# Reading the DeltaNet's triangular systems from plain scratch with six loads a step, and handing out no late modulation at the end of the attention

## The chip, the cores and the metric

The kernel runs on one core of one Trainium2 chip. The metric is the time of one execution in device microseconds (us). Before the change it is 1784.63 us, the median of 3 runs (1782.84 to 1789.32).

The core's engines run side by side, each through its own list of instructions in order: TensorE (PE, matmuls; PEld is its loading of weights), VectorE (DVE), ScalarE (ACT) and GpSimd (POOL). The queue of SyncE (SP) and that of ScalarE issue the transfers (DMAs).

## What is computed

One layer over 256 latent tokens and 256 context tokens of width 2048, in fp32. Cut to what matters here:

```python
sh1, sc1, g1, sh2, sc2, g2 = split(silu(c) @ w_ada + b_ada, 6)     # and the same for c_ctx
(lq_a, lkv_a, lk_r, ldq, ldk, ldv, ldz, lda, ldb, lga, lgb) = split_columns(
    modulate(rmsnorm(x, norm_mix), sh1, sc1) @ w_in)               # and the same for ctx
...
y_mla_l = attend_latent(q_l, k_l, v_l, k_c, v_c)
o_dn_c, s_ctx = dn_bidirectional(cq, ck, cv, cgd, cbeta, s_zero, not last)
o_dn_l, _ = dn_bidirectional(lq, lk, lv, lgd, lbeta, s_ctx, True)
y_l = merge_branches(y_mla_l, dn_output(o_dn_l, ldz, dn_o_norm, x.dtype), lga, lgb, w_o_mla, w_o_dn, w_out)
x = x + g1 * y_l
x = x + g2 * conv_glu(modulate(rmsnorm(x, norm_ffn), sh2, sc2), w_ffn_up, ffn_conv, w_ffn_down)
```

The part that the change touches is the gated DeltaNet. For each of 8 heads, 2 directions and 8 chunks of 64 tokens (4 of the context, 4 latent) it solves one unit lower triangular system of size 64:

```python
kb = k * beta
m = where(strict, einsum('bhnid,bhnjd->bhnij', kb, k) * decay, 0.0)
rhs = concatenate([v * beta, kb * exp(gc)[..., None]], axis=-1)
sol = triangular_solve(m + eye(c), rhs, left_side=True, lower=True, unit_diagonal=True)
u, w = sol[..., :dv], sol[..., dv:]
...
def step(s, inp):
    v_new = u_c - einsum('bhcd,bhde->bhce', w_c, s)
    s_next = s * g_c + einsum('bhcd,bhce->bhde', k_c, v_new)
    o = einsum('bhcd,bhde->bhce', q_c, s) + einsum('bhcj,bhje->bhce', a_c, v_new)
    return s_next, o
```

## The kernel before, in words

**Weights.** Every weight block of 128x1024 comes from HBM in fp32 (512 KB, tile `raw`), through a ring of NR = 8 tiles. ScalarE casts it to a high part (`whi`, L123), VectorE subtracts that from it for a low part (`wlo`, L124), and TensorE multiplies with both, from rings of NH = 6. A weight can be requested as soon as a `raw` tile is free, and the requests stand in SP's queue in the order in which they were planned. The 128 blocks of the "late modulation" (`rawa`, the four of the six modulation vectors that are not needed at the start) go through the same ring.

**Order.** TensorE's order is pinned to the program's; ScalarE's, VectorE's and SP's follow the scheduler except where they are pinned. A transfer counts up one of eight completion counters when it lands. The transfers of SP's queue and of ScalarE's queue take these eight in turn, and a transfer whose counter was last given to one still under way waits for that one: the rows of the order below show it as a wait for DMAHW0 to DMAHW7.

**The stages, with the times of the profile.** (1) The start, to 35 us: SP loads the vectors, x (`xl`) and the context (`xc`), then 16 MB of scale weights (`wt`) and 16 MB of shift weights (`raw<-in_wadab`), of each of which the first parts are needed first. TensorE adds up the squares (`pss`, the norms), the shifts (`amp`), and then projects (`fp`, `mmp`). ScalarE's copy of `amp` leads to `shs`, which gives the modulated input `h` of the first projection. (2) The DeltaNet's heads, to about 440 us. They leave, for each of the 128 systems (4x32), its two 32x32 diagonal blocks in scratch in HBM (`Ud`) and the block below the diagonal (`Uo`). (3) The attention, from about 440 to 740 us, in four pairs of heads, `b = 0` to 3, each with 7 rounds `n`. Its own work is handed out in pieces (`mla_project`, `mla_attend`). With every piece of estimated cost `c`, `side(c, r)` hands out other work that is due: `fill` (the projections of z and of the gates, tiles `raw<-in_wz` and `in_wgm`), `inv` (the triangular systems) and `ada` (the late modulation, AD = 0.55 of the cost). In the last pair the ratio is 2.0 for fill and inv, and behind the loop stands one more call, `side(2600, 1.0)`. (4) The scan over the eight chunks, about 735 to 890 us, with the attention's out projection (`branch`) and the gate tiles between its steps, and `ada` at ADS = 0.3 of the cost. (5) The out projection, the norm and the feed-forward, to the end. `ada` is handed out there too, until all four quarters are done.

**The systems.** `inverse()` loads `Ud` into `ux` and solves the diagonal blocks on VectorE. It then stores them: 8 transfers to `Xq` (L846, for each of four groups of partitions the transposed first block `xt` and the second block), and 16 transfers to `Tt` (L851), in which each system stands as it will be multiplied, as a 64x64 matrix in two 32x32 diagonal blocks: pieces of 32 numbers, 128 bytes. `ux` lives in a pool that is closed behind it, and its place in memory is given to tiles of the attention. `off_diagonal()` then takes the systems in eight steps: it loads `uo` (from `Uo`) and the two inverse diagonal blocks `xd` (from `Xq`, L869), multiplies them (`ivp`), and stores the block beside the diagonal to `Tt`, in 4 transfers a step from SP (L892). The fourth block of each system is zero: it is written to `Tt` at the start from a small zero tile `none`, in two transfers of 2048 pieces from ScalarE's queue (L656). In the scan, `load_system` (L1273) loads a step's 16 systems into `tt` with one transfer, 128 rows of 2 KB; two tiles `tt` are used in turn. TensorE's `yp` multiplies with them.

**The attention's keys.** `k_norm` (L1029) sums the squares of a key tile over the partitions (`ks`: TensorE, from ScalarE's `ksq`), and VectorE makes `km` from it (L1035). In the first pair `km` lies where `ux` lay.

**The late modulation.** `ada_rest()` loads 128 blocks `rawa` (L262) and multiplies each with the spread conditioning vector on VectorE, summing along the row (L281; the same operation appears under L68 where its place was pinned). Two loads are requested ahead of the product. They form four quarters of 32 products (`ada.done` counts them), of which the first must be complete ahead of the out projection (`wout`) and the third ahead of the feed-forward.

**What the change touches**: L101 and L102, L653 to L656, `inverse()` L846 to L851, `off_diagonal()` L869 and L892, `side` (L1179), its two calls (L1209 and L1212), the scan's tiles (L1259) and `load_system` (L1273). In the changed kernel the same lines stand 2 to 11 lower: L127 there is L129 here, L842 is L846, L860 is L869, L1269 is L1273.

## Time and profile before

| | |
|---|---|
| median of 3 runs | 1784.63 us (1782.84 to 1789.32) |
| the profiled execution | 1786.89 us |
| its span in the trace | 1785.1 us |
| TensorE's mean granted clock | 0.985 |
| TensorE matmul (PE) busy | 1737.5 us |
| TensorE weight load (PEld) busy | 1507.2 us |
| VectorE (DVE) busy | 1356.8 us |
| ScalarE (ACT) busy | 950.5 us |
| GpSimd (POOL) busy | 41.4 us |
| moved by DMA | 417.15 MB, HBM 232 GB/s over the span |

How to read the rows in the prediction. A row that begins with two numbers is of the timeline: the time from the span's start, the duration (us), the engine, the line, the operation, the tile that is written and the tiles read. A number with an arrow in brackets is the idle time of the engine ahead of it and what ended it. A row "A <- B: total, times, longest" is of the waits: what A waited for B in all, how often, and the longest. A row that begins with two times and a colon is a stretch: its length, then the busy time of PE, PEld, DVE, ACT and POOL in it with the number of instructions, the granted clock, the mean busy share of the 16 DMA engines, and GB/s. Rows with "min/median/max" are of one line's or one tile's instructions: count, durations in ns, first and last time. L68 is the line of a helper through which the pinned instructions of all engines go, so these are told apart by their tiles.

### The profile page before, as it was taken

How to read it: one execution, taken by the hardware profiler on the slowest of the kernel's cores; microseconds unless marked ns; L12 is line 12 of the kernel's file. 1: busy time of each engine (PE TensorE's matmuls, PEld its weight loads, DVE VectorE, ACT ScalarE, POOL GpSimd, SP SyncE). 2: the span in 40 equal slices, each digit the busy share in tenths (PEclk: the TensorE clock that was granted, in tenths of full speed). 3: DMA queues.
4: the chain of work that ended last, by engine and by line, in shares of the span. 5: the costliest groups of instructions: out<-in, count | busy, mean ns of one | idle time of the engine just before them, and what ended most of it. 6: DMA issues, size and time to landing. Idle time of an engine off the chain costs nothing.

```text
span 1785.1 us, 34155 instructions
## 1 busy us (share of the span) xinstructions
PE 1737.5 (97%) x12957; PEld 1507.2 (84%) x12957; DVE 1356.8 (76%) x2696; ACT 950.5 (53%) x1966; POOL 41.4 (2%) x48
## 2 busy tenths in 40 slices
PE   7999999999799999999999999999999999999999
PEld 5887888888688888788878888888888888888888
DVE  4677799879578879787779979887788887655554
ACT  3335454454477766665646546555555555544443
POOL 0000011000000000000010000000000000000000
PEclk8999999999899999999989999999999999999999
DMA  9992588783578868999647968776667776666662
GB/s 348 407 373 93 150 235 249 230 257 109 138 255 248 260 214 273 360 339 361 233 130 233 328 199 281 232 237 207 202 219 229 228 225 201 182 198 199 198 199 87
DMA packets 190260, 417.15 MB, mean 234 GB/s; under 512 B 56912, under 2 KB 95696, under 8 KB 187792
## 3 DMA queue, kind: packets, MB, share of 16 engines
q1 hardware_dynamic: 165024, 401.59, 68.7%
q10 hardware_dynamic: 25072, 13.39, 2.5%
q8 instruction: 101, 1.65, 0.4%
q14 instruction: 63, 0.52, 0.1%
HBM read 387.00 MB, written 27.79 MB: 232 GB/s over the span
## 4 chain that ended last, share of the span: by engine, by line
PE 63%; issue 8%; DMA 1%; DVE 1%; ACT 0%; SPq 0%; POOL 0%; POOLq 0%; DVEq 0%
PE fps L68 27%; PE dps L68 13%; PE gtp L68 11%; PE brp L68 3%; PE vps L68 1%; PE kps L68 1%; PE qps L68 1%; PE sps L68 1%; PE kp L68 1%; PE ivp L68 1%; PE op L68 1%; PE yps L68 1%; PE yp L68 0%; DMA YM<-Ys 0%; SPq L851 0%
## 5 line engine op out<-in xcount | busy, mean ns | idle before, releaser
L123 ACT CAST whi<-raw 128x512 fp32r<-128x512 f32 (+1 forms) x940 | 578.9, 620 | 413.6 <-PE dps L68 113.5
L124 DVE TENSOR_TENSOR wlo<-raw,whi 128x512 fp32r<-128x512 f32 (+1 forms) x940 | 637.3, 686 | 211.4 <-ACT whi L123 203.5
L68 PE MATMUL fps<-H,whi 128*128 128x512 f32 x1376 | 475.0, 394 | 3.1 <-DVE H L1472 3.1
L68 PE MATMUL fps<-H,wlo 128*128 128x256 f32 x1376 | 372.3, 280 | 0.0
L68 PEld LDWEIGHTS fps<-H,whi 128*128 128x128 f32 x1376 | 253.7, 189 | 54.7 <-issue 1.9
L68 PEld LDWEIGHTS fps<-H,wlo 128*128 128x128 f32 x1376 | 259.7, 189 | 7.5 <-DVE wlo L124 0.5
L68 PE MATMUL gtp<-h,whi 128*128 128x512 f32 x640 | 231.4, 399 | 0.0
L68 PE MATMUL mmp<-h,whi 128*128 128x512 f32 x640 | 229.5, 400 | 0.0
L68 PE MATMUL dps<-GB,whi 128*128 128x512 f32 (+1 forms) x595 | 195.7, 377 | 0.0
L68 PE MATMUL mmp<-h,wlo 128*128 128x256 f32 x640 | 177.5, 283 | 0.0
L68 PE MATMUL gtp<-h,wlo 128*128 128x256 f32 x640 | 173.9, 282 | 0.0
L68 PE MATMUL dps<-GB,wlo 128*128 128x256 f32 x560 | 155.2, 282 | 0.0
L68 PEld LDWEIGHTS gtp<-h,whi 128*128 128x128 f32 x640 | 120.5, 190 | 25.3 <-issue 0.9
L68 PEld LDWEIGHTS mmp<-h,whi 128*128 128x128 f32 x640 | 119.8, 189 | 24.9 <-ACT dkx L531 0.3
L68 PEld LDWEIGHTS dps<-GB,whi 128*128 128x128 f32 x595 | 109.2, 188 | 20.2
L68 PEld LDWEIGHTS gtp<-h,wlo 128*128 128x128 f32 x640 | 121.5, 190 | 4.5
L68 PEld LDWEIGHTS mmp<-h,wlo 128*128 128x128 f32 x640 | 121.8, 190 | 3.6 <-issue 1.4
L68 PEld LDWEIGHTS dps<-GB,wlo 128*128 128x128 f32 x560 | 105.8, 189 | 0.6
L281 DVE CUSTOM_DVE_ANT_0 rawa<-rawa,sch 128x1024 f32<-128x1024 f32 x68 | 82.9, 1222 | 20.9 <-DMA rawa<-in_wada 19.4
L68 PE MATMUL fp<-h,gh 128*128 128x256 f32 (+1 forms) x448 | 85.5, 291 | 2.5 <-ACT h L68 1.7
L68 PEld LDWEIGHTS fp<-h,gh 128*128 128x128 f32 (+1 forms) x448 | 69.7, 190 | 7.6 <-issue 4.1
L68 DVE CUSTOM_DVE_ANT_0 rawa<-rawa,sch 128x1024 f32<-128x1024 f32 x60 | 72.9, 1218 | 0.0
(574 smaller groups left out, 2563.4 us busy)
## 6 DMA issues: line engine op xcount, KB each, us to landing
rawa<-in_wada SPq DMA_DIRECT2D x128, 512.0 KB, 5.2
raw<-in_wgate SPq DMA_DIRECT2D x82, 512.0 KB, 4.4
raw<-in_wval SPq DMA_DIRECT2D x82, 512.0 KB, 4.6
raw<-in_wdown SPq DMA_DIRECT2D x80, 512.0 KB, 4.2
wt<-in_wadas SPq DMA_DIRECT2D x16, 1024.0 KB, 9.6
raw<-in_wadab SPq DMA_DIRECT2D x32, 512.0 KB, 11.6
raw<-in_wgm SPq DMA_DIRECT2D x32, 512.0 KB, 5.6
raw<-in_wgd SPq DMA_DIRECT2D x32, 512.0 KB, 6.9
```

The costliest lines, as they stand in the source:

```text
L68: i = f(*a, **k)
L123: act.copy(hi, raw)
L124: dve.tensor_tensor(out=lo, in0=raw, in1=hi, op=ALU.subtract)
L281: (odve if ada.bound else dve).tensor_tensor_reduce(out=w, in0=w, in1=sch, scale=1.0, scalar=0.0, op0=ALU.mult, op1=ALU.add, accum_out=par ...
```

## The change

The scratch `Tt` is dropped, and with it the zero tile, the two zero fills at the start, the 16 transfers behind `inverse()` and the 4 a step in `off_diagonal()`. `Xq` gets a third plane: the transposed first block, the first block as it is, and the second. That makes 12 transfers behind `inverse()`; `off_diagonal()` reads planes 0 and 2. Its result goes to a new scratch `Xo` in one transfer a step, from ScalarE's queue. In the scan two `tt` tiles are zeroed once on GpSimd, and `load_system` fills the three blocks of each system with six transfers of 32 KB (two directions by three blocks; 256 pieces of 128 bytes each), from `Xq[1]`, `Xq[2]` and `Xo`. And `side` has a flag `late` that leaves out `ada`: it is set for `b == 3 and n > 3`, which is three of the seven rounds (4, 5 and 6) of the last pair, and for the call behind the loop. The two edits are independent of each other, and no computation is changed.

```diff
--- before.py
+++ after.py
@@ -98,8 +98,6 @@
     make_identity(nc, ident)
     ones = const.tile([P, 1], F32, name="ones")
     dve.memset(ones, 1.0)
-    none = const.tile([P, 32], F32, name="none")
-    pool.memset(none, 0.0)
     onesr = const.tile([P, P], F32R, name="onesr")
     dve.tensor_copy(onesr, ones.broadcast_to([P, P]))
     half = const.tile([P, 1], F32, name="half")
@@ -650,10 +648,8 @@
     Ud = dram.tile([4, 32, 2, 32, 32], F32, name="Ud")
     Uo = dram.tile([4, 32, 32, 32], F32, name="Uo")
 
-    Xq = dram.tile([2, 32, 4, 32, 32], F32, name="Xq")
-    Tt = dram.tile([P, 16, 4, 64], F32, name="Tt")
-    for d in range(2):
-        act.dma_start(Tt[64 * d + 32 : 64 * d + 64, :, :, 0:32].rearrange("c s g j -> c (s g) j"), none[:32].unsqueeze(1).broadcast_to([32, 64, 32]))
+    Xq = dram.tile([3, 32, 4, 32, 32], F32, name="Xq")
+    Xo = dram.tile([32, 4, 32, 32], F32, name="Xo")
     As = dram.tile([4, P, 8, 64], F32, name="As")
     conv = mid.tile([P, 24, 3], F32, name="conv")
     dve.tensor_scalar(out=conv, in0=off["dn_conv"].rearrange("p (f w) -> p f w", w=3), scalar1=0.5, scalar2=None, op0=ALU.mult)
@@ -842,13 +838,8 @@
         act.copy(xt, X[:, 0].rearrange("p c j -> p j c"))
         for g in range(4):
             gs = slice(32 * g, 32 * g + 32)
-            for n, x in enumerate((xt, X[:, 1])):
+            for n, x in enumerate((xt, X[:, 0], X[:, 1])):
                 sync.dma_start(Xq[n, :, g], x[gs])
-        for g in range(4):
-            for d in range(2):
-                for b in range(2):
-                    rs = slice(64 * d + 32 * b, 64 * d + 32 * b + 32)
-                    sync.dma_start(Tt[rs, :, g, 32 * b : 32 * b + 32].rearrange("c s j -> s c j"), X[32 * g + 16 * d : 32 * g + 16 * d + 16, b])
         yield 1000
         pI.close()
 
@@ -866,7 +857,7 @@
             sync.dma_start(uo, Uo[:, :, rs].rearrange("g j r i -> (g j) r i"))
             xd = pi.tile([P, 2, 4, 32], F32, tag="xd", name="xd", bufs=2)
             for n in range(2):
-                sync.dma_start(xd[:, n], Xq[n, rs].rearrange("r g j c -> (g j) r c"))
+                sync.dma_start(xd[:, n], Xq[2 * n, rs].rearrange("r g j c -> (g j) r c"))
             return uo, xd
 
         ahead = load(0)
@@ -887,9 +878,7 @@
                 if n == 0:
                     yield OC / 2
             act.copy(uo, ip)
-            for g in range(4):
-                dst = Tt[64 * (q // 4) : 64 * (q // 4) + 32, 4 * (q % 4) : 4 * (q % 4) + 4, g, 32:64]
-                sync.dma_start(dst, uo[32 * g : 32 * g + 32])
+            act.dma_start(Xo[4 * q : 4 * q + 4].rearrange("r g c i -> (g c) r i"), uo)
             yield OC / 2
         pI.close()
 
@@ -1176,10 +1165,11 @@
     pairs = {}
     ryx = mid.tile([P, 2, T], F32, tag="krd", name="ryx")
 
-    def side(c, r):
+    def side(c, r, late=False):
         fill(r * c)
         inv(r * c)
-        ada(AD * c)
+        if not late:
+            ada(AD * c)
 
     pe.pinned = True
     for c in mla_project(0):
@@ -1206,10 +1196,10 @@
             for st in (pr, tail, at):
                 c = next(st, None)
                 if c is not None:
-                    side(c, R1 if b < 3 else 2.0)
+                    side(c, R1 if b < 3 else 2.0, b == 3 and n > 3)
             next(back, None)
         tail = at
-    side(2600, 1.0)
+    side(2600, 1.0, True)
     for _ in tail:
         pass
     inv.finish()
@@ -1258,6 +1248,8 @@
         jit = ps1.tile([P, 6, 1024], F32, name="jit")
         TTv = [ps1.tile([P, HEADS, 64], F32, name=f"tt{n}") for n in range(2)]
         av = ps1.tile([P, HEADS, 64], F32, name="av")
+        for n in range(2):
+            pool.memset(TTv[n], 0.0)
         half_ = [slice(0, 64), slice(64, 128)]
         S = ps1.tile([P, HEADS, 2, P], F32, name="S")
         steps = (4, 5, 6, 7, 0, 1, 2, 3)
@@ -1270,7 +1262,11 @@
 
         def load_system(n):
             st, tt = steps[n], TTv[n % 2]
-            sync.dma_start(tt, Tt[:, 2 * st : 2 * st + 2].rearrange("p a g j -> p (a g) j"))
+            for d in range(2):
+                for r, c, x in ((0, 0, Xq[1]), (32, 32, Xq[2]), (0, 32, Xo)):
+                    rs, cs = slice(64 * d + r, 64 * d + r + 32), slice(c, c + 32)
+                    n = 16 * d + 2 * st
+                    sync.dma_start(tt[rs, :, cs], x[n : n + 2].rearrange("a g c i -> c (a g) i"))
             return tt
 
         def load_ke(n):
```

How the instructions move is told by the order of each engine. A row names the line, the operation, the tile written, the tile read and its size; brackets hold the completion counters or engines that it must wait for by the program. The first place is the start of ScalarE's queue, where the zero fills stood. Before:

```order
L306 DMA cv<-in_cv 128x32
L321 DMA sel<-in_sel 128x3
L656 DMA Tt<-none 2048x1x32 [waits Pool_49]
L309 ACT_TABLE_LOAD
L309 ACTIVATE cth<-cv 128x32 [waits DMAHW0_49]
L68 ACTIVATE sq<-xl 128x4x256 [waits DMAHW3_49]
L68 ACTIVATE sq<-xl 128x4x256 [waits DMAHW6_49]
L656 DMA Tt<-none 2048x1x32
```

The same place now:

```order
L304 DMA cv<-in_cv 128x32
L319 DMA sel<-in_sel 128x3
L307 ACT_TABLE_LOAD
L307 ACTIVATE cth<-cv 128x32 [waits DMAHW0_49]
L68 ACTIVATE sq<-xl 128x4x256 [waits DMAHW3_49]
L68 ACTIVATE sq<-xl 128x4x256 [waits DMAHW5_49]
```

Both fills are gone from ScalarE's queue; as they took two of the eight counters in turn, the counters of all later transfers of both queues change. The second place is SP's queue at the end of `inverse()`, from its last copies to `Xq` on. `raw<-in_wz` is a weight of the z projection, `xd` what `off_diagonal()` reads. Before:

```order
L846 DMA Xq<-xt 32x1024
L846 DMA Xq<-ux 32x1024
L851 DMA Tt<-ux 16x32x32 x16
L869 DMA xd<-Xq 128x4x32 x4
L129 DMA raw<-in_wz 128x1024
L262 DMA rawa<-in_wada 128x1024
L129 DMA raw<-in_wqb 128x1024
```

The same place now:

```order
L842 DMA Xq<-ux 32x1024 x2
L842 DMA Xq<-xt 32x1024
L842 DMA Xq<-ux 32x1024 x2
L860 DMA xd<-Xq 128x4x32 x2
L127 DMA raw<-in_wz 128x1024
L860 DMA xd<-Xq 128x4x32 x2
L260 DMA rawa<-in_wada 128x1024
```

The 16 transfers from `ux` to `Tt` no longer stand ahead of `xd` and of the weights; the weight of z is requested between the loads of `xd`. The third place is SP's queue at the head of the scan: `jit` are its keys and values, `tt` its systems. Before:

```order
L1267 DMA jit<-KTs 128x1024
L1268 DMA jit<-Vs 128x1024
L1273 DMA tt_8909<-Tt 128x512
L1278 DMA jit<-KEs 128x1024
L1267 DMA jit<-KTs 128x1024
L1268 DMA jit<-Vs 128x1024
```

The same place now:

```order
L1259 DMA jit<-KTs 128x1024
L1260 DMA jit<-Vs 128x1024
L1269 DMA tt_8860<-Xq 32x8x32 x2
L1269 DMA tt_8860<-Xo 32x8x32
L1269 DMA tt_8860<-Xq 32x8x32 x2
L1269 DMA tt_8860<-Xo 32x8x32
L1274 DMA jit<-KEs 128x1024
L1259 DMA jit<-KTs 128x1024
```

Six transfers stand where one stood, in the first and in each later step. TensorE's order is the same before and after.

## Prediction

> **What bounds the kernel now.** I read the page first, then the waits of TensorE, then its busy time by stretches, and then the timeline at each stretch where it stands.
>
> ```profile
> PE 1737.5 (97%) x12957; PEld 1507.2 (84%) x12957; DVE 1356.8 (76%) x2696; ACT 950.5 (53%) x1966; POOL 41.4 (2%) x48
> PE ks L68 <- DVE km L1035: 6.5, 1, 6.5
> PE pss L68 <- DVE sq L68: 4.9, 4, 3.9
> PE yps L68 <- DVE PT L124: 3.5, 1, 3.5
> 500.00:550.00 50.00, 50.00 (x412) 44.18 (x411) 40.65 (x91) 36.15 (x86) 3.50 (x3) 1.00 0.80 251
> ```
>
> TensorE is busy 97% of the span. No matmul is added, dropped or reordered, so only its idle time and the slow-clock time behind it can change. Where nothing stands out (500 to 550), it is busy 50.00 of 50. The idle time is 1785.1 - 1737.5 = 47.6 us, and these three waits, 14.9 of it, lie where the change works: the start (`pss`), the first keys (`ks`) and the end of the attention (`yps`).
>
> **The start: two zero fills go.** The queue of SP loads x (`xl`) and the context (`xc`), then what modulation and the first projection need. The first row is SP's waits, the next six the timeline, the last two the stretches (mean clock, DMA share, GB/s at the end).
>
> ```profile
> SPq L68 <- DMA Tt<-none: 9.7, 1, 9.7
> 5.57 0.33 SPq L68 DMA_DIRECT2D xl<-in_xT  x1
> 15.58 0.33 SPq L68 DMA_DIRECT2D xc<-in_ctxT  x1
> 21.14 1.81 PE L68 MATMUL pss<-sq,ones 128*32 128x512 f32 x8 [3.90 <-DVE sq L68]
> 30.60 1.93 PE L68 MATMUL amp<-raw,csf 128*32 128x256 f32 x32
> 33.45 0.42 ACT L68 ACTIVATE shs<-amp,vecs 128x2 f32<-128x2 f32 x2 [0.43 <-PE amp L68]
> 35.13 0.53 PE L68 MATMUL fp<-h,gh 128*96 128x256 f32 x1 [1.75 <-ACT h L68]
> 16.00:18.00 2.00, 1.24 (x12) 0.97 (x8) 0.00 (x0) 0.15 (x1) 0.00 (x0) 1.00 0.80 153
> 30.00:35.00 5.00, 2.42 (x64) 1.50 (x64) 1.17 (x3) 2.88 (x9) 0.00 (x0) 1.00 1.03 426
> ```
>
> The last quarter of the context is issued at 15.58, though the load ahead of it went at 5.57: SP waits 9.7 us until the first zero fill, issued from ScalarE's queue, has landed. VectorE squares that quarter for `pss`, so TensorE stands 3.90. SP's order shows why: loads of both queues take eight completion counters in turn, and that load's counter is the fill's. Before, then after:
>
> ```order
> L68 DMA xl<-in_xT 128x1024 [waits DMAHW2_49]
> L68 DMA xc<-in_ctxT 128x1024 [waits DMAHW4_49]
> L68 DMA wt<-in_wadas 128x2048 [waits DMAHW5_49]
> ```
>
> ```order
> L68 DMA xl<-in_xT 128x1024 [waits DMAHW1_49]
> L68 DMA xc<-in_ctxT 128x1024 [waits DMAHW2_49]
> L68 DMA wt<-in_wadas 128x2048 [waits DMAHW3_49]
> ```
>
> The load now waits for the counter of a small early load and can go at about 6. From there the start is a matter of bytes: the last shift weights stand behind 8.6 MB (x and context 4.2, scale weights 2.1, shift weights 2.1, vectors 0.2). At about 0.41 MB/us, a little under the 426 GB/s row, from 2 us on, they are in by 23; with an estimated tail of 1 to 1.5 us (the smallest landing below is 1.9 with its issue) it is 24 to 24.5. Now they end with the `amp` matmuls at 30.60 to 32.5; then those would end at about 25.5. The chain from there to the first projection (`shs` at 33.45, `fp` at 35.13) is the same. That is 7 us early; I take 6.5, since loads for later steps are led by a little less. The lower bound is 4, the wait of 3.9 alone; the upper 7.5.
>
> **The first keys: 16 writes of Tt go.** The solved diagonal blocks lie in `ux`. Before, SP stores them to Xq in 8 writes and to Tt in 16 of 128-byte pieces. The first four rows are the timeline, then the stretches around it.
>
> ```profile
> 460.33 17.87 SPq L851 DMA_DIRECT2D Tt<-ux  x16
> 480.60 0.16 DVE L1035 SCALAR_TENSOR_TENSOR km<-ks,krm 128x4 f32<-128x4 f32 x1 [10.91 <-DMA xd<-Xq]
> 480.91 0.60 PE L68 MATMUL ks<-ones,ksq 128*32 128x1 f32 x32 [6.51 <-DVE km L1035]
> 485.75 0.62 ACT L123 CAST whi<-raw 128x512 fp32r<-128x512 f32 x1 [12.81 <-DMA raw<-in_wz]
> 469.00:471.30 2.30, 0.11 (x3) 0.01 (x2) 0.69 (x2) 1.19 (x4) 0.00 (x0) 1.00 0.08 27
> 471.30:474.40 3.10, 3.10 (x44) 2.79 (x44) 0.00 (x0) 1.49 (x3) 0.00 (x0) 0.59 0.28 49
> 474.40:480.90 6.50, 0.01 (x1) 0.02 (x1) 0.30 (x2) 0.00 (x0) 0.00 (x0) 0.50 0.70 89
> 480.90:485.50 4.60, 4.59 (x49) 4.39 (x50) 2.67 (x7) 0.00 (x0) 2.01 (x2) 0.50 0.88 222
> L846 SPq DMA_DIRECT2D Xq<-ux x4: 339/418/436, 454.0 to 459.9; - x4
> DMA to landing us min/median/max: 1.9/2.7/3.2
> ```
>
> VectorE's `km` is the first tile to reuse the place of `ux`, and so waits for all reads of it. TensorE makes its sums from 471.3, so it could run at 471.9, but it runs at 480.60, when the last Tt write has landed (the row names the transfer that came nearest). TensorE's second `ks` stands behind it for 6.51 us. The weights of z are queued behind the same writes, and ScalarE idles 12.81 us for them. On SP, after the change (before, the 16 Tt rows stand where the third Xq copy ends and `xd` begins):
>
> ```order
> L842 DMA Xq<-ux 32x1024 [waits DMAHW2_49]
> L842 DMA Xq<-ux 32x1024 [waits DMAHW3_49]
> L860 DMA xd<-Xq 128x4x32 [waits DMAHW5_49,DMAHW4_49,DMAHW0_49]
> L860 DMA xd<-Xq 128x4x32
> L127 DMA raw<-in_wz 128x1024 [waits DMAHW6_49,DVE_49]
> ```
>
> Eight Xq writes go between 454.0 and 459.9; four more at 0.42 us end at about 462 and land 2.7 later, before 465. Then `km` runs at 471.9, under TensorE's twelve `vps` matmuls (to 474.4), and the second `ks` follows with no gap: 6.5 us off the path. The weights of z go out at about 465 instead of 480.88 and are in before TensorE needs them at about 480. What is late next is the wait of 2.2 us ahead of the first `ks` (the stretch from 469): ScalarE's order there is the same, so it stays. The clock: after it the granted clock is 0.59 for 3.1 us, then 0.50 for 4.6 us after the big wait, which costs 1.3 + 2.3 = 3.6 us. I leave 2 us of that for the wait that stays (4 us at half clock), so 1.5 more is saved. The term is 8.0 us; bounds 6.5 and 6.5 + 3.6 = 10.1.
>
> The Trainium skill, "TensorE: Matmul & The Clock Gate" (What's actually happening), says that the clock halves after an idle window of about 3.4 us. By that rule the stall of 2.2 us alone would not slow it and this term would be 10.1 us, the sum 15.6; here the clock fell to 0.59 within 3 us of that stall, which speaks against it.
>
> **Tt's last columns: 32 writes become 8 on ScalarE's queue.** SP loses 32 issues where TensorE has no gap (500 to 550), so nothing is gained. ScalarE gets 8 issues, and SP can wait for one of them on a shared counter.
>
> ```profile
> L910 ACTq DMA_DIRECT2D Gs<-zx x18: 326/326/333, 550.5 to 735.5; - x18
> SPq L262 <- DMA Gs<-zx: 3.9, 1, 3.9
> ```
>
> 8 x 0.33 = 2.6 us of ScalarE beside 36 of 50 busy; at worst one SP wait of 3.9. I take 0.5 us, between 0 and 3.9.
>
> **The scan: 48 loads in place of 8.** Each of 8 steps read 128 pieces of 2 KB; now it reads 6 x 256 = 1536 pieces of 128 bytes. The nearest rows for such pieces are the Tt writes (window 461 to 478); then the old loads, their first use, a zeroing of tiles as large as the new one, SP's largest waits in the scan, a load and the use of what it brings, and two stretches.
>
> ```profile
> q1 hardware_dynamic: 7156, 1.06, 46.9%
> L1273 SPq DMA_DIRECT2D tt<-Tt x8: 319/326/510, 721.7 to 845.1; - x8
> L68 PE MATMUL yp<-jit,tt x32: 269/269/320, 739.6 to 740.4; 64*64 64x128 f32 x32
> 437.50 0.99 POOL L861 MEMSET bd<- 128x512 f32 x2 [38.61 <-PE mmp L68]
> SPq L129 <- DVE wlo L124: 31.2, 21, 4.8
> SPq L1267 <- PE kp L68: 21.3, 5, 6.9
> 742.08 0.42 SPq L1273 DMA_DIRECT2D tt<-Tt  x1
> 779.85 1.03 PE yp L68 x32
> 740.00:760.00 20.00, 20.00 (x203) 17.07 (x192) 15.71 (x34) 15.16 (x39) 0.00 (x0) 1.00 1.00 371
> 860.00:880.00 20.00, 20.00 (x291) 17.38 (x290) 12.66 (x29) 11.78 (x31) 0.00 (x0) 1.00 0.53 178
> ```
>
> A small piece took 17 x 16 x 0.469 / 7156 = 17.8 ns of an engine, so a step's load takes 1.7 us of all 16, eight take 13.7; the old ones took 2.1 MB at 400 GB/s, 5.2. That adds 8.5 us of transfers to a stretch whose share is 1.00 early and 0.53 late. SP gets 40 more issues of 0.42, 17 us, where two rows alone show it waiting 52 us for buffers. A system loaded at 742.08 is multiplied at 779.85, so the loads have 37 us, and the first, issued at 721.7 for a use at 739.6, some 15 behind the zeroing (0.5 us a tile by `bd`). Cost: 0.5 us, between 0 and 4.
>
> **The late modulation: out of the last pair.** The condition holds for rounds 4 to 6 and the call behind them. By VectorE's order 66 of the 128 products stood ahead of the scan's second step; now 63 do.
>
> ```profile
> 717.83 1.22 DVE L68 CUSTOM_DVE_ANT_0 rawa<-rawa,sch 128x1024 f32<-128x1024 f32 x1
> 719.72 1.86 PE L68 MATMUL yps<-PT,V 128*128 128x512 f32 x8 [3.52 <-DVE PT L124]
> 710.00:720.00 10.00, 6.03 (x36) 4.92 (x36) 10.00 (x22) 7.78 (x18) 0.00 (x0) 1.00 0.79 222
> 1200.00:1400.00 200.00, 200.00 (x1154) 175.81 (x1154) 159.37 (x309) 111.19 (x217) 0.00 (x0) 1.00 0.68 216
> ```
>
> VectorE is full for the ten microseconds in which TensorE waits 3.52 for the last `PT`. On VectorE, between the last two `PT`, before and after:
>
> ```order
> L124 TENSOR_TENSOR PT<-ptp,PT 128x4x128
> L124 TENSOR_TENSOR wlo<-raw,whi 128x512
> L520 TENSOR_TENSOR ryx<-yps,ryx 128x256
> L124 TENSOR_TENSOR wlo<-raw,whi 128x512
> L124 TENSOR_TENSOR YM<-ryx,YM 128x256
> L520 TENSOR_TENSOR zx<-gtp,zx 128x256
> L68 ISA rawa,parts<-rawa,sch 128x1024
> L68 ISA parts 128x1
> L124 TENSOR_TENSOR PT<-ptp,PT 128x4x128
> ```
>
> ```order
> L122 TENSOR_TENSOR PT<-ptp,PT 128x4x128
> L518 TENSOR_TENSOR ryx<-yps,ryx 128x256
> L122 TENSOR_TENSOR wlo<-raw,whi 128x512 x2
> L122 TENSOR_TENSOR YM<-ryx,YM 128x256
> L518 TENSOR_TENSOR zx<-gtp,zx 128x256
> L122 TENSOR_TENSOR wlo<-raw,whi 128x512
> L122 TENSOR_TENSOR PT<-ptp,PT 128x4x128
> ```
>
> The product between them has gone, but it stands earlier now: counted from the start, 60 products lie ahead of the last `PT` in both. The three that leave came after it, where TensorE had no gap. Term 0, between -3.5 and +1. They land in the feed-forward, 3.7 us of VectorE beside 159 of 200 busy: nothing.
>
> **The sum.** -6.5 - 8.0 + 0.5 + 0.5 + 0 = -13.5 us. The profiled execution took 1786.89 us (span 1785.1), 2.3 above the median of 1784.63. From the median, 1771.1; the profiled one would be near 1773.4. About 0.5%, 8.9 us, is what a measurement here can tell from no change.
>
> **Rivals.** *Only the keys' stall goes* (chance 0.12): the earlier context only meets the next full queue, as a DMA share of 1.03 at 30 to 35 could mean; against it, 153 GB/s at 16 to 18 shows capacity lost. -8 + 1 = -7: 1777.6. *The stall moves* (0.08): `km` is freed, but the start gives only its lower bound and the next weights eat the clock's part and more: -4 - 2.5 + 1 = -5.5, 1779.1. *More goes* (0.13): the clock stays up (-10.1) and the `yps` wait goes too (-3.5): with -6.5 and +1, -19.1: 1765.5. *Slower* (0.05): the six loads hold up the weights behind them on SP. Its price is 5 more issues a step at the pace of the Tt writes, 17.87 / 16 = 1.12 us, so 5.6 us a step, 39 over seven steps: 1784.6 - 14.5 + 39 = 1809. It decides once such a delay exceeds the lead of a weight load on its use, and against it stand SP's waits for buffers.
>
> The Trainium skill's "DMA: Bandwidth & Descriptors" (Rules for kernel authors) advises joining small transfers, under 64 KB one pays mostly overhead; the new loads are 32 KB, and by it the slower case would be the one to fear. No run so far shows such loads in the scan.
>
> **How the numbers follow.** My own case has 0.62. Its terms' bounds and the rivals give 1765 to 1779. Faster by over 0.5%: most of the own case, the larger gain and a little of the first rival, 0.74; the same, 0.21; slower, 0.05.
>
> **What would show it.** Right: the last `xc` issued near 6 and `fp` near 28.5; no wait of `ks` on `km`, `km` near 465 on the new time; TensorE full in the scan; the `yps` wait still some 3 us. Wrong: a new wait for `raw` ahead of `fp`, in the scan, or at the gate tiles after the first keys.

## The result, and the profile after

The changed kernel takes 1774.6 us (median of 11 executions, 1770.04 to 1780.3 but for one of 6182.54 at a mean clock of 0.379, which the ratio leaves out); the kernel before took 1784.85 beside it. The ratio is 0.9938, 95% interval 0.9925 to 0.9951: 11 us faster, where 13.5 were forecast. A second session gave 0.9949 (0.9936 to 0.9963). The forecast of 1771.1 was 3.5 us too low; the measured time lies inside the range of 1765 to 1779.

The profiled execution is the slowest of those ten: 1780.3 us, span 1778.5, clock 0.988 (the one of 1770.04 had 0.994). Its span is 6.6 us under that of before. Since TensorE's order is the same in both, the gain can be followed matmul by matmul. First the page's busy times and the waits of TensorE after the change:

```profile
PE 1735.7 (98%) x12957; PEld 1502.4 (84%) x12957; DVE 1352.9 (76%) x2696; ACT 946.1 (53%) x1966; POOL 42.8 (2%) x49
```

```profile
PE ptp L68 <- ACT s__8497 L1125: 3.3, 1, 3.3
PE gtp L68 <- DVE wlo L122: 2.7, 3, 1.6
PE ks L68 <- ACT ksq L1013: 2.2, 1, 2.2
PE yps L68 <- DVE PT L122: 1.9, 1, 1.9
PE pss L68 <- DVE sq L68: 0.7, 3, 0.3
```

The 6.5 us of `ks` for `km` are gone and `pss` waits 0.7 in place of 4.9. In their place stand two waits that were hardly there before or not at all: `ptp` for a softmax scaling (0.5 before) and `gtp` for `wlo`.

The timeline after the change, at the start, the first keys and the end of the attention:

```profile
5.48 0.60 SPq L68 DMA_DIRECT2D xc<-in_ctxT  x1
29.58 0.53 PE L68 MATMUL fp<-h,gh 128*96 128x256 f32 x1 [1.75 <-ACT h L68]
453.96 1.24 SPq L842 DMA_DIRECT2D Xq<-ux  x2
465.47 0.43 PE L68 MATMUL ks<-ones,ksq 128*32 128x1 f32 x32 [2.19 <-ACT ksq L1013]
465.98 0.16 DVE L1024 SCALAR_TENSOR_TENSOR km<-ks,krm 128x4 f32<-128x4 f32 x1 [2.10 <-PE ks L68]
467.46 0.43 PE L68 MATMUL ks<-ones,ksq 128*32 128x1 f32 x32
691.35 0.62 ACT L121 CAST YM<-YM 128x512 fp32r<-128x512 f32 x1 [3.79 <-DMA YM<-Ys]
691.87 0.72 ACT L1125 ACTIVATE s__8497<-s__8497,mns 128x512 f32<-128x512 f32 x1
692.64 0.66 PE L68 MATMUL ptp<-ident,s__8497 128*128 128x128 f32 x4 [3.34 <-ACT s__8497 L1125]
707.13 1.24 PE L68 MATMUL yps<-PT,V 128*128 128x512 f32 x3 [1.87 <-DVE PT L122]
```

The last context load goes at 5.48 (before 15.58) and the first `fp` runs at 29.58 (35.13). `km` follows its sums by half a microsecond. At 691 ScalarE stands 3.79 us at a cast of `YM` whose load has not landed; the scaling `s` is queued behind that cast, and TensorE's `ptp` behind `s`. Before, the same cast stood behind `s`. The rows of before that answer to the first `ks` and to `ptp`:

```profile
471.29 0.43 PE L68 MATMUL ks<-ones,ksq 128*32 128x1 f32 x32 [2.19 <-ACT ksq L1024]
704.52 0.60 PE L68 MATMUL ptp<-ident,s__8537 128*128 128x128 f32 x4
```

The matmuls of one tile are the other view used: `yp`, the scan's product with the systems, with the first and the last time behind the durations. Before, all but the first step:

```profile
L68 PE MATMUL yp<-r,tt x224: 269/269/320, 759.0 to 892.6; 64*64 64x128 f32 x112
```

And after the change, the first step and the others:

```profile
L68 PE MATMUL yp<-jit,tt x32: 269/269/320, 727.0 to 727.8; 64*64 64x128 f32 x32
L68 PE MATMUL yp<-r,tt x224: 269/269/320, 746.4 to 885.7; 64*64 64x128 f32 x112
```

The same instruction in both, and what was gained between one place and the next:

| place | before | after | lead | gained here | forecast |
|---|---|---|---|---|---|
| first `fp` | 35.13 | 29.58 | 5.55 | 5.5 | 6.5 |
| first `ks` | 471.29 | 465.47 | 5.82 | 0.3 | 0 |
| second `ks` | 480.91 | 467.46 | 13.45 | 7.6 | 8.0 (with the clock behind it) |
| last `ks` | 653.7 | 638.3 | 15.4 | 2.0 | in the 8.0 |
| a `ptp` at the attention's end | 704.52 | 692.64 | 11.88 | -3.5 | -0.5 (the writes of `Tt`) |
| last `yps` with a wait | 719.72 | 707.13 | 12.59 | 0.7 | 0 |
| first `yp` | 739.6 | 727.0 | 12.6 | 0 | 0 |
| last `yp` | 892.6 | 885.7 | 6.9 | -5.7 | -0.5 |
| end of the span | 1785.1 | 1778.5 | 6.6 | -0.3 | 0 |

The row of the last `ks` is read from these two views, before and after (first and last time behind the durations):

```profile
L68 PE MATMUL ks<-ones,ksq x256: 170/170/210, 471.3 to 653.7; 128*32 128x1 f32 x128
L68 PE MATMUL ks<-ones,ksq x256: 170/170/191, 465.5 to 638.3; 128*32 128x1 f32 x128
```

Up to the scan the kernel is 12.6 us ahead, where the terms of the forecast give 14.0. The scan, from first to last `yp`, takes 158.7 us where it took 153.0 (892.6 - 739.6). That length, taken within one execution, is the measure in what follows; for the attention it is the time from the first to the last `ks`, 172.8 us after and 182.4 before.

What holds up the scan is seen on SP and on ScalarE (timeline of SP in one step, then a wait of ScalarE and one of SP in the scan):

```profile
729.69 1.11 SPq L1269 DMA_DIRECT2D tt<-Xq  x2
731.25 0.30 SPq L1269 DMA_DIRECT2D tt<-Xo  x1
732.51 1.67 SPq L1269 DMA_DIRECT2D tt<-Xq  x2
735.06 0.30 SPq L1269 DMA_DIRECT2D tt<-Xo  x1
736.33 0.35 SPq L127 DMA_DIRECT2D raw<-in_wgd  x1
```

```profile
ACT whi L121 <- DMA raw<-in_wgd: 12.8, 8, 4.6
SPq L1269 <- DMA jit<-Vs: 4.8, 5, 1.2
```

Six loads hold SP from 729.69 to 736.33, 6.6 us, though each is issued in a third to half a microsecond: between them SP waits for the completion counters of loads that are still under way. The last row is one of these waits of SP in the scan; the six rows of its kind come to 24 us. The weights of the next gate tile are behind them, and ScalarE waits for these, 12.8 us in all; before, ScalarE waited for no weight there. No time is lost in the first two steps, though: to the first `yp` of the third step both kernels take 40.2 us. The 5.7 us go in the steps behind it.

### The profile page after: what moved, and what is told of

It reads as the page before. It is cut to its first block, busy times and chain, and to the rows that moved or that the text cites. A ratio compares the mean times of both kernels' runs of the same rounds, so it can differ in the third digit from the quotient of the medians.

```text
span 1778.5 us, 34182 instructions
## 1 busy us (share of the span) xinstructions
PE 1735.7 (98%) x12957; PEld 1502.4 (84%) x12957; DVE 1352.9 (76%) x2696; ACT 946.1 (53%) x1966; POOL 42.8 (2%) x49
## 4 chain that ended last, share of the span: by engine, by line
PE 53%; issue 19%; DVE 1%; DMA 1%; ACT 0%; POOL 0%; POOLq 0%; ACTq 0%; DVEq 0%; SPq 0%
PE fps L68 26%; PE dps L68 13%; PE gtp L68 6%; PE vps L68 1%; PE kps L68 1%; PE qps L68 1%; PE sps L68 1%; PE ivp L68 1%; PE yps L68 1%; DMA YM<-Ys 0%; DVE wlo L122 0%; PE ptp L68 0%; DMA Ys<-ryx 0%; PE kbp L68 0%; POOL om L173 0%
```

## The experiments

Ratios are to the kernel before on the same chip, with 95% intervals. The scan's length is from the first to the last `yp` of the profiled execution.

| run | loads a step | late edit | ratio | scan, us |
|---|---|---|---|---|
| before | one | no | 1 | 153.0 |
| late_only | one | yes | 1.0045 (1.003 to 1.0061) | 158.8 |
| scratch_only | six | no | 0.9981 (0.9967 to 0.9995) | 163.7 |
| after | six | yes | 0.9938 (0.9925 to 0.9951) | 158.7 |
| after_again | six | yes | 0.9949 (0.9936 to 0.9963) | 157.7 |
| scan_one | one, other data | yes | 0.9946 (0.9926 to 0.9967) | 155.5 |
| scan_one_nolate | one, other data | no | 0.9895 (0.9881 to 0.991) | 153.0 |
| scan_small_nolate | one of small pieces, other data | no | 0.9938 (0.9915 to 0.9961) | 154.5 |
| scan_pool | six from GpSimd | yes | 1.001 (0.9997 to 1.0023) | 173.2 |
| after_fills | six | yes | 0.9988 (0.9974 to 1.0002) | 158.7 |
| after_ttwrites | six | yes | 1.0006 (0.9993 to 1.0019) | 158.7 |
| late_back | six | yes, cast later | 0.9946 (0.9933 to 0.9959) | 158.9 |
| one_from_scratch | one | no | 1.003 (1.0016 to 1.0045) | 153.0 |
| one_assembled | one | no | 0.9964 (0.995 to 0.9978) | 153.0 |

**The late edit alone.** To the kernel before:

```diff
-        ada(AD * c)
+        if not late:
+            ada(AD * c)
...
-                    side(c, R1 if b < 3 else 2.0)
+                    side(c, R1 if b < 3 else 2.0, b == 3 and n > 3)
...
-    side(2600, 1.0)
+    side(2600, 1.0, True)
```

> The kernel before with the late modulation edit alone; scratch, zero fills and loads as before. Theory (from the two traces): the edit costs time. Without the modulation products the scheduler puts ScalarE's first cast of the attention's read-back heads (YM) ahead of the softmax scaling s, and that cast waits for its load; TensorE's ptp then waits some 3.3 us with 1.7 us of slow clock behind it, while the last wait for PT shrinks by about 1.7. So +1 to +4 us on before: ratio 1.0005 to 1.0025, with a ptp wait of 2 us or more in its profile. Rival: the edit is neutral and the ptp wait in the changed kernel came from its scan or its earlier start; then ratio 1.000 within 0.0005 and no ptp wait over 1 us.

Measured: 1792.01 against 1783.37 us, 8 us slower, more than the theory had. Its `ptp` wait is there (the first fence, TensorE's waits). There is a second cost, which neither theory had, in the scan: VectorE's products wait for their own loads. The next fence is VectorE's wait in the scan of late_only, then come its `yp`, and last the same wait before the change.

```profile
PE ptp L68 <- ACT s__8537 L1136: 2.7, 1, 2.7
```

```profile
DVE rawa L281 <- DMA rawa<-in_wada: 27.0, 15, 3.4
```

```profile
L68 PE MATMUL yp<-jit,tt x32: 269/269/320, 737.3 to 738.1; 64*64 64x128 f32 x32
L68 PE MATMUL yp<-r,tt x224: 269/269/321, 756.7 to 896.1; 64*64 64x128 f32 x112
```

```profile
DVE rawa L281 <- DMA rawa<-in_wada: 5.8, 5, 1.7
```

VectorE works in order. While it stands at a product, the scan's own `r` and `S`, on which the next step hangs, stand behind it: 27.0 us in place of 5.8, and the scan takes 5.8 us longer.

**The changed kernel without the late edit.** The `if not late:` is taken out of `side` again.

> The changed kernel without the late modulation edit: the scratch, the loads and the start are the new ones. Theory: 2 to 5 us faster than the changed kernel, about 1770 to 1772, ratio 0.991 to 0.993 to before; no wait of ptp over 1 us, and the last yps wait for PT back at about 3.5 us. Rival (the edit is neutral): the same as the changed kernel, ratio 0.9938 within 0.0015.

Measured: 0.9981, 6 to 8 us slower than the changed kernel in its two sessions, where the theory had it faster. The theory is wrong on this: with the new scratch the edit gains time, though alone it costs 8 us. The `ptp` wait is gone and `yps` waits 3.5 again, as expected; the loss is in the scan, 163.7 us (TensorE's waits in it, then `yp`):

```profile
PE gtp L68 <- DVE wlo L122: 3.3, 7, 1.7
PE gtp L68 <- ACT whi L121: 2.0, 2, 1.7
```

```profile
L68 PE MATMUL yp<-jit,tt x32: 269/269/320, 723.4 to 724.2; 64*64 64x128 f32 x32
L68 PE MATMUL yp<-r,tt x224: 269/269/320, 743.8 to 887.1; 64*64 64x128 f32 x112
```

Of the 10.7 us that this scan is longer than before, 4.8 go in its first two steps (45.0 us in place of 40.2), in which the changed kernel loses nothing; the rest is about what the changed kernel loses too. So the edit's gain lies at the head of the scan. SP's timeline fits that: ahead of the first load of `tt`, scratch_only has requested 156 weights and 63 products, the changed kernel 158 and 61. The 160th weight is then requested 15.1 us after the first `yp` in scratch_only, 9.3 in the changed kernel. In the profiled executions the changed kernel is only 1.4 us ahead at the last `yp` (3.8 in its second profile), since it reaches the scan later; where the rest of the 6 to 8 us of the times lies isn't shown.

**One load a step.** To the changed kernel, in `load_system`; the scan multiplies with data of the right size that are not the systems:

```diff
-            for d in range(2):
-                for r, c, x in ((0, 0, Xq[1]), (32, 32, Xq[2]), (0, 32, Xo)):
...
+            sync.dma_start(tt, As[st % 4])
```

> The changed kernel with a single 256 KB load of 2 KB pieces a step in the scan, from another scratch of that size (As), in place of the six; the systems multiplied in the scan are therefore not the solved ones, all else is done. Theory: the 5.2 us of small TensorE waits for wlo in the scan come from the six loads, which wait for completion counters on SP's queue ahead of the weights; they go, and the kernel is 4 to 6 us faster than the changed one, ratio 0.9905 to 0.992. Rival: those waits come from the modulation products or the earlier arrival at the scan; then they stay and the ratio is 0.9938 within 0.0015.

Measured: 0.9946, the same as the changed kernel. The waits for `wlo` did go, and the scan is 3 us shorter (155.5), but the time is not: the theory's sum fails here. In this scan VectorE waits 20.1 us for the loads of its products, where it waited 2.7 in the changed kernel: what late_only showed is back. Then the same without the late edit:

> The changed kernel with one 256 KB load a step in the scan (from As, so the systems in the scan aren't the solved ones) and without the late modulation edit. The edit alone cost the kernel before 0.45 per cent and gained the changed kernel 0.43. Theory: it is the six loads that it makes up for; with one load it has nothing to make up for, so without it the kernel gains all of the start and the keys, 13 to 15 us on before: ratio 0.9915 to 0.993, 8 us or more faster than the same with six loads (0.9981), and TensorE full in the scan. Rival: the edit's worth hangs on when the scan starts and not on the loads; then 0.996 to 0.999.

Measured: 0.9895, 1768.57 us, the fastest of all, and faster than the theory had. VectorE's waits for its products' loads are 8.6 us, and the scan takes 153.0 us, as before the change:

```profile
L68 PE MATMUL yp<-jit,tt x32: 269/269/321, 722.9 to 723.7; 64*64 64x128 f32 x32
L68 PE MATMUL yp<-r,tt x224: 269/269/321, 742.3 to 875.9; 64*64 64x128 f32 x112
```

The four together show how the two edits bear on each other. Without the late edit the six loads cost 0.0086 of the time, 15 us (10.7 of them in the scan of the profiled executions; by the intervals of the two ratios the 15 are uncertain by some 4). With it they cost nothing that the times show and 2 to 3 us of the scan. The edit costs 8 to 9 us with one load and gains 6 to 8 with six: each is bad for a kernel without the other.

**The changed kernel once more.**

> The changed kernel once more, on the chip of the three that follow, as their measure. Theory (the six loads a step starve the weights): in its profile TensorE again waits 2 us or more for wlo in the scan, ScalarE's casts wait for weights, and SP waits on the counters of other loads ahead of tt; the ratio to before is 0.992 to 0.9955. Rival (the first profile was an odd one): no such waits, at the same ratio.

Measured: 0.9949. TensorE waits 2.2 us for `wlo` in the scan (1.8 for the gates, 0.4 for the branches), ScalarE 7.8 us for weights, and the scan takes 157.7 us; the first profile wasn't an odd one in this.

**Issues or pieces.** One load a step of 2048 pieces of 128 bytes, without the late edit:

```diff
+            sync.dma_start(tt.rearrange("p h (c j) -> p (h c) j", c=2), KTs[st].rearrange("p h (c j) -> p (h c) j", j=64)[:, :, 0:32])
```

> One load a step in the scan, as in the run with one load and without the late modulation edit, but in 2048 pieces of 128 bytes (taken from KTs, so the systems in the scan aren't the solved ones) in place of 128 pieces of 2 KB. It tells the issues from the pieces. Theory: the six loads cost 15 us because each issue stands on SP's queue and waits for a counter ahead of the weights; with one issue the small pieces cost 0 to 3 us: ratio 0.9895 to 0.9915. Rival: the pieces hold up the weights on the DMA engines; then 0.995 to 0.999, near the six loads.

The scan's length (`yp` again) answers it:

```profile
L68 PE MATMUL yp<-jit,tt x32: 269/269/320, 726.6 to 727.4; 64*64 64x128 f32 x32
L68 PE MATMUL yp<-r,tt x224: 269/269/321, 746.0 to 881.1; 64*64 64x128 f32 x112
```

It is 154.5 us, 1.5 more than with 2-KB pieces, while six loads with fewer pieces take 10.7 more. So in the scan it is mostly the six issues, not the pieces. The times leave it open: 0.9938 lies between the two expectations, with an interval that reaches from one into the other. The profiled execution is 3.8 us longer than that with large pieces (spans 1772.0 and 1768.2), but it was 3.8 us behind at the first `ks` already (466.4 and 462.6), long ahead of any of these loads.

**The six loads from GpSimd.** In `load_system`, `sync.dma_start` becomes `pool.dma_start`.

> The changed kernel with the six loads a step issued from GpSimd's queue in place of SP's; all else and the result are the same. Theory: SP's queue no longer waits on counters for them, the weights come as early as with one load, and the waits for wlo in the scan go: 1 to 5 us faster than the changed kernel, ratio 0.991 to 0.993. Rival 1: it is the small pieces on the DMA engines that hold up the weights, not SP's queue; then the waits stay and the ratio is that of the changed kernel. Rival 2: GpSimd issues so slowly that yp waits for tt; then slower than the changed kernel, 0.996 or more.

The time is that of the second rival, 1.001, but not by its mechanism: no `yp` waits for `tt`. The scan takes 173.2 us (first `yp` at 719.0, last at 892.2), some 5 us of it through three stretches of half clock, 3.4 us each. SP is free of the loads and ScalarE waits for no weight, but VectorE waits for its products' loads 48.2 us, and TensorE for what is queued behind them (the waits in the scan):

```profile
DVE rawa L279 <- DMA rawa<-in_wada: 48.2, 16, 6.1
PE yp L68 <- DVE r L1304: 6.3, 3, 2.3
```

It is the mechanism of late_only, larger. Why the products' loads come later still when SP is free isn't shown.

**The terms of the start and of the keys, undone.** The zero fills come back at the start, into a scratch that nothing reads:

> The changed kernel with the two zero fills back at the start, into a scratch that nothing reads. Theory: the 5.5 us that the first projection came earlier are lost again, +5 to +6.5 us on the changed kernel, ratio 0.9968 to 0.9978, with the fourth context load issued near 15.5 us. Rival: the start's gain is swallowed by the next full queue or by slow-clock slots that fall elsewhere; then +0 to +2, ratio 0.9938 to 0.995.

Measured: 0.9988, 7 to 9 us slower than the changed kernel, more than the theory had. SP waits as before (its wait, then the fourth context load in the timeline, then the matmuls of `fp`, whose first time is behind the durations):

```profile
SPq L68 <- DMA Tt<-none: 10.0, 1, 10.0
```

```profile
15.86 0.33 SPq L68 DMA_DIRECT2D xc<-in_ctxT  x1
```

```profile
L68 PE MATMUL fp<-h,gh x448: 277/280/526, 34.9 to 144.4; 128*128 128x256 f32 x128, 128*96 128x256 f32 x22
```

`fp` comes 5.3 us later than in the changed kernel, an amount that the intervals of the two ratios hold. And the 16 writes of `ux` come back, into such a scratch:

> The changed kernel with the 16 writes of 128-byte pieces behind the diagonal blocks back, into a scratch that nothing reads; its 12 writes to Xq stay too. Theory: the stall of the first keys returns (ks waits 6 us or more for km, and a slow clock behind it), 8 to 10 us slower than the changed kernel: ratio 0.9985 to 1.000. Rival: the stall came from the order of the weights of z behind them and is covered now; then 0.994 to 0.996.

Measured: 1.0006, 10 to 12 us slower. The stall is back, and longer; the 16 writes take 19.39 us where they took 17.87 (timeline):

```profile
453.66 19.39 SPq L848 DMA_DIRECT2D Tt<-ux  x16
475.83 0.61 PE L68 MATMUL ks<-ones,ksq 128*32 128x1 f32 x32 [9.90 <-DVE km L1030]
```

From the first to the last `ks` it takes 184.6 us (463.9 to 648.5), 10 to 12 more than in the changed kernel's two profiles (172.8 and 174.3).

**The cast that waits.** In `heads_back` the first cast is handed out two rounds later, so that it comes behind `s`:

```diff
         yield
         yield
+        yield
+        yield
         for q in range(3):
```

> The changed kernel with the first cast of the read-back heads (YM) handed out two rounds later, so that on ScalarE it stands behind the softmax scaling s that TensorE's ptp waits for. Theory: the ptp wait of 3 us and its slow clock go, 2 to 4 us faster than the changed kernel, ratio 0.9915 to 0.993. Rival: the wait moves to the last PT, whose cast now stands behind those of YM; then yps waits 3 us or more and the ratio is that of the changed kernel, 0.9938 within 0.0015.

The rival: the `ptp` wait is gone, the ratio is 0.9946, and TensorE's wait for the last `PT` is as long as before the change:

```profile
PE yps L68 <- DVE PT L122: 3.4, 1, 3.4
```

The lateness of ScalarE and VectorE at this place shows at one matmul or at the other.

**Two versions meant to beat both.** Both read each step with one load from `Tt` and leave out the late edit. In the first, `off_diagonal()` copies the blocks from the planes of `Xq` to `Tt`, HBM to HBM, in seven transfers a step from SP:

```diff
+            for b in range(2):
+                sync.dma_start(Tt[lo + 32 * b : lo + 32 * b + 32, ss, :, 32 * b : 32 * b + 32].rearrange("c s g j -> c (s g) j"), Xq[1 + b, 4 * q : 4 * q + 4].rearrange("s g c j -> c (s g) j"))
```

> A version meant to beat both, with the reference's result: the scan reads each step's systems with one load from Tt, as before the change; Tt is put together in HBM from the new planes of Xq in the eight steps of the blocks beside the diagonal (7 transfers a step from SP: two copies from Xq, one of zeros, four of the solved block), so that neither the zero fills at the start nor the writes that held ux are there, and the late modulation edit is left out. Theory: as the run with one load and without that edit, 0.9895, plus 0 to 2 us for 24 more transfers where SP waits for buffers anyway: ratio 0.989 to 0.992. Rival: these transfers, from HBM to HBM in 128-byte pieces, hold the counters that SP and ScalarE need and the weights come late in the attention; then a wait for wlo between 490 and 690 us, 0.993 or more.

The rival: 1.003. From the first to the last `ks` it takes 190.4 us (465.0 to 655.4), 16 to 18 more than in the changed kernel's two profiles. TensorE is busy 193.47 of 205 us between 510 and 715 (199.79 in the changed kernel), and SP stands at the solved block (SP's waits between 440 and 700, then that stretch):

```profile
SPq L885 <- ACT uo L882: 27.1, 6, 9.0
```

```profile
510.00:715.00 205.00, 193.47 (x1438) 165.72 (x1438) 154.00 (x337) 128.74 (x295) 10.32 (x9) 0.99 0.75 240
```

In the second, ScalarE's queue stores the block as in the changed kernel, and eight large copies put `Tt` together, such as:

```diff
+                    sync.dma_start(Tt[rs, :, :, c : c + 32].rearrange("c s g j -> c (s g) j"), x[16 * d : 16 * d + 16].rearrange("s g c j -> c (s g) j"))
```

> A second version meant to beat both, with the reference's result. As in the last one, the scan reads each step's systems with one load from Tt and the late modulation edit is left out. But the blocks beside the diagonal go to Xo by one transfer a step from ScalarE's queue, as in the changed kernel, and Tt is put together by eight large transfers from SP, one a step from the second step on (zeros, the two diagonal blocks from Xq, the last block from Xo; 2048 pieces of 128 bytes each). The last version lost about 15 us between 510 and 715 us with SP waiting 27 us for the solved block (uo). Theory: it was those waits at the head of SP's queue; without them TensorE is nearly full there and the kernel comes near the run with one load and without the edit: ratio 0.9895 to 0.993. Rival: it was the copies from HBM to HBM themselves, which hold up the weights; then TensorE loses 8 us or more between 510 and 715 us again, ratio 0.996 or more.

The rival again: 0.9964. It is faster than before, but not faster than the changed kernel. Its scan is full (153.0 us), while the attention takes 182.6 us from the first to the last `ks` (468.7 to 651.3), 8 to 10 more than in the changed kernel's two profiles. TensorE waits 3.2 us for casts of the gates' weights there, with 6.8 us of slow clock behind the longest of these waits, and ScalarE waits for these weights:

```profile
ACT whi L123 <- DMA raw<-in_wgm: 10.4, 6, 3.7
```

These 10.4 us are only 2.8 more than in the changed kernel (7.6), so whether the copies themselves or their place in SP's queue hold TensorE up isn't shown. Both versions pay in the attention what they save in the scan, and the 0.9895 of the run without the systems was not reached by a kernel with them; two versions don't show that none could.

## Why the prediction was right, and where its sum was off

*What bounds the kernel.* Right in the main: TensorE's idle time and slow clock moved. (In the scan, 3.3 of the 5.7 us are idle time; the other 2.4 stand in TensorE's busy time, 155.4 us in place of 153.0.) Between 490 and 680 us it stays full after the change, so the 32 writes that became 8 on ScalarE's queue cost nothing (0.5 was taken).

*The start.* Right in mechanism, 1 us too large: 5.5 us at the first `fp`, between the bounds of 4 and 7.5 (3.9 in the second profile, whose first `fp` is at 31.2). Putting the fills back undoes it.

*The first keys.* Right: 7.6 us to the second `ks` and 2.0 more behind it, where the clock stays up. That is 9.6 us, between the 8.0 taken and the 10.1 of its bound; in the second profile it is 8.1. The prediction held that the wait of 2.2 us, which stays, slows the clock by itself, and left 2 us for it. In the first profile it did not, in the second it did (the last section has both): this part of the term is chance.

*The scan.* This step failed: 0.5 us, between 0 and 4, became 5.7 in the profiled execution, and without the late edit 10.7. The prediction priced the issues rightly in its slower rival (5.6 us a step for five more; the timeline shows 5.2 to 8.2 for six) but set SP's old waits for buffers against them as cover. They are a cover in part only. At the head of the scan two systems are loaded one behind the other, and no weight is requested for 18.8 us (scratch_only) or 24.7 (after), where 10.8 was the longest such pause there before; scratch_only loses 4.8 us there. Behind it both lose some 6 us more, where ScalarE waits for weights that stand behind the six. The rival's mechanism was there; that it came to 6 or 11 us and not 39 fits with SP's slack. On coalescing, the Trainium skill's "DMA: Bandwidth & Descriptors" (Rules for kernel authors) was the better guide: the six loads of 32 KB cost the scan 10.7 us, and one of 256 KB, even in pieces of 128 bytes, costs it 1.5.

*The late edit.* This step failed too. It was set at 0 because VectorE's order ahead of the last `PT` was counted; ScalarE's order was not looked at, and there the scheduler had moved the cast of `YM` ahead of `s`. And its main effect lies neither there nor in the feed-forward but in the scan, through the order of loads on SP. Alone it costs 8 us; with six loads it gains 6 to 8. What fits the gain is that two more weights and two fewer products are requested ahead of the scan, which bridges SP's stall in the first two steps; no run changed that number by itself.

So that the sum came within 3 us is luck in part. Two terms that the text put near nothing are large and of opposite sign in the time: the six loads cost some 15 us, and the late edit gives some 7 back. And without both of them the gain is 19 us (0.9895; 17 by the spans of the profiled executions), where the terms of the start and of the keys were set at 14.5.

## What to carry to other kernels

Many small loads in place of one are paid at the head of the queue that issues them, as waits for completion counters ahead of whatever is queued behind, and are found by asking what that queue must deliver next, not by its mean slack. When optional work is withheld, read the new order on every engine and queue, not only on the engine that did the work: a cast that waits for its load, or a product whose load comes late, stops all that is behind it. And two edits that come together are tested in all four combinations; here the late edit changed its sign, and the six loads cost 15 us without it and nothing that the times show with it.

## What the runs showed of the hardware

The granted clock falls to half for stretches of about 3.4 us or a multiple, after partly idle stretches, and which of these it falls after differs between executions. Stretches of before, with the clock third from the right; the second, at half clock, follows one in which TensorE was busy 2.47 of 4 us:

```profile
154.00:158.00 4.00, 2.47 (x18) 2.05 (x17) 3.47 (x13) 1.25 (x3) 0.00 (x0) 0.98 0.35 131
158.00:161.20 3.20, 3.20 (x10) 1.88 (x9) 2.83 (x6) 0.00 (x1) 0.00 (x0) 0.50 0.00 0
```

In the changed kernel the same matmuls come 7 us earlier, at full clock (first row). Near 440 us it is slow where before was not, and around and behind the wait of 2.2 us at 465 it is not slow where before was:

```profile
151.00:154.40 3.40, 3.40 (x18) 2.05 (x17) 3.07 (x8) 1.05 (x3) 0.00 (x0) 1.00 0.00 0
437.80:444.50 6.70, 6.16 (x22) 5.26 (x22) 5.02 (x13) 2.35 (x5) 0.81 (x1) 0.50 0.20 73
465.50:468.90 3.40, 3.40 (x85) 3.23 (x86) 2.31 (x7) 2.35 (x5) 1.01 (x1) 1.00 0.44 123
```

In its second profile, behind the same wait (there at 464 to 466), the clock did fall:

```profile
467.00:470.40 3.40, 3.40 (x46) 3.16 (x45) 2.79 (x8) 1.87 (x4) 1.01 (x1) 0.50 0.61 158
```

Of eleven profiles in which this wait stands with no longer one close behind it, the clock fell for 3.4 us within a microsecond of it in six (after_again, scratch_only, scan_one, late_back, one_from_scratch, one_assembled) and not in the other five.

Each such stretch costs about 1.7 us (3.4 at half speed). Across ten executions of the changed kernel the time runs from 1770.04 us at a mean clock of 0.994 to 1780.3 at 0.988; 0.006 of 1775 us is 10.7 us of clock, about the whole spread. The Trainium skill's "TensorE: Matmul & The Clock Gate" (What's actually happening) has the window run freely, whatever the kernel does, and differ from run to run; the rows agree with that. Its condition, an idle window of about 3.4 us, doesn't agree: the clock fell behind a stretch that was busy for 2.47 of 4 us. A profiled execution therefore carries some 5 us of chance either way here, and a term of that size is read from the length of its own stretch or from many executions, not from one span.
